# Hybrid layer on one core: 512-wide products, rests at every fourth column, low parts on GpSimd

## The chip, the core and the metric

The kernel runs on one NeuronCore of a Trainium2 chip. Its engines work side by side, each through its own queue in program order: TensorE (PE; PEld is its loading of the stationary operand), VectorE (DVE), ScalarE (ACT), GpSimd (POOL) and SyncE (SP, here only issuing DMAs). They wait for each other by semaphores. The metric is the device time of one execution in microseconds.

## What is computed

One hybrid layer on 256 tokens of width 2048, in float32. The normalised input goes through one wide projection, whose columns feed three branches; their results are gated, projected, summed, and projected once more.

```python
h = rms_norm(x, norm_g); mem_n = rms_norm(mem, mem_norm_g)
proj = h @ w_in                                   # 2048 x 20672
# split: qkv_a, z_a (1536 each), rkv_b, z_b (1536 each), lw, la (96), q_c, z_c (1024), gates (3 x 2048)
y_a = attention(q_a, k_a, v_a, rel_bias) * silu(z_a)          # 12 heads of 128, causal, with a bias by distance
y_b = rwkv7_time_mix(r_b, k_b, v_b, lw, la, ...) * silu(z_b)  # 24 heads of 64, a recurrence over the tokens
y_c = memory_cross_attention(q_c, mem_n, w_mem_kv) * silu(z_c)  # 4 heads of 256
g_a, g_b, g_c = split(sigmoid(gates), 3)
merged = g_a * (y_a @ w_proj_a) + g_b * (y_b @ w_proj_b) + g_c * (y_c @ w_proj_c)
return rms_norm(x + merged @ w_out, final_norm_g)
```

## The kernel before

**Products in two parts.** Weights and activations are float32. Each is split into a high part (fp32r) and a low part (what the high part leaves), and a product is high by high plus high by low plus low by high. Activations are kept as `[128, tile of the depth, 2, 256]`: the high and low part of 256 tokens stand next to each other.

**Jobs and chunks.** A `Job` is a product of an activation with 256 columns of a weight matrix. It goes through the depth in chunks of `KC = 4` tiles of 128 rows (512 KB). Each chunk goes through three steps, in `issue_dma` (SP loads `raw`, three buffers), `issue_split` (ACT copies the high part into `wt`, L265; VectorE subtracts to get the low part, L268; four buffers), and `products` (TensorE). `prefetch(i, ...)` keeps splits three chunks ahead of the products of chunk `i`. In mode "fm" the weights are stationary; a tile of 128 x 128 weights takes a pair: the high part by 512 columns (both parts of the activation, L303), and the low part by 256 columns (L304). In mode "tm" activations are stationary and weights stream, in the same pair. The last job of the kernel alone uses three products of 256 columns (L301). `take` adds the two halves of the bank at a job's end: ACT copies one half to `et` (L312), then VectorE or GpSimd adds.

**Lanes.** All other work (attention, the recurrence, activations) is written as generators, the lanes. After the products of each chunk `step_lanes` lets each lane issue its next piece; `yield n` is a rest of n chunks. So the program's order on every engine is set by how chunks and pieces interleave. `force` and `drain` run lanes without chunks in between, when something is needed at once or a stage ends. A lane sets flags for others, such as "attn" (the attention of a group is done) or "state_free" (the recurrent state of a group is ready).

**Stages.** The first stage (196 chunks) makes the columns for the first two branches, for six groups of two pairs of heads: jobs R, K, V, Z of the recurrence, and Q, K, Z, V of the attention. The second makes the memory branch (chunks 196 to 259), the third the gates and projections, the fourth the output. `open_p2` drains the lanes at the end of the first stage.

**The recursion.** In `rw_lane` a group needs the inverses of 8 triangular blocks per partition quadrant. Blocks go through DRAM into `NB`, and VectorE runs 31 columns, each with products (L658, into `fs_t`) and sums (L662, into `X`). A rest follows every fifth column, in which VectorE's queue gets the low part of the next chunk. Later pieces make the state, turn `YT` to tokens (L769), normalise (L772 to L798: `gn_m`, `gn_v`, square root on ACT at L134, `rs_rg`, then `Y`, with one product on GpSimd at L791), turn `Y` back (L806) and multiply into `yb`. In `attn_a` the weights of the attention are turned (L854) and copied by ACT to `pT` (L855), then multiplied with `va` (L861, L863).

## Time and profile before

| | |
|---|---|
| median of 3 runs | 1492.12 us (1491.28 to 1493.12) |
| the profiled execution | 1491.59 us, span 1489.9 us |
| TensorE busy | 1457.5 us (98%), 9083 products |
| VectorE / ACT / GpSimd busy | 981.8 / 791.3 / 199.3 us |
| low parts on VectorE (L268) | 451, 1244 ns in the mean |
| high parts on ACT (L265) | 452, 1055 ns in the mean |
| loads of weights | 448 of 512 KB and 4 of 384 KB, some 4 us from issue to landing |

A busy time is the union of an engine's instructions. Products on TensorE overlap in their records, so the step from start to start tells their pace, not the mean duration. Idle time of an engine costs only where the bounding engine waits for it. Line numbers are those of the kernel before, in the diff's removed lines and in all rows of it.

### The profile page before, as it was taken

How to read it: one execution, taken by the hardware profiler on the slowest of the kernel's cores; microseconds unless marked ns; L12 is line 12 of the kernel's file. 1: busy time of each engine (PE TensorE's matmuls, PEld its weight loads, DVE VectorE, ACT ScalarE, POOL GpSimd, SP SyncE). 2: the span in 40 equal slices, each digit the busy share in tenths (PEclk: the TensorE clock that was granted, in tenths of full speed). 3: DMA queues.
4: the chain of work that ended last, by engine and by line, in shares of the span. 5: the costliest groups of instructions: out<-in, count | busy, mean ns of one | idle time of the engine just before them, and what ended most of it. 6: DMA issues, size and time to landing. Idle time of an engine off the chain costs nothing.

```text
span 1489.9 us, 24099 instructions
## 1 busy us (share of the span) xinstructions
PE 1457.5 (98%) x9083; PEld 1249.5 (84%) x9083; DVE 981.8 (66%) x1978; ACT 791.3 (53%) x1261; POOL 199.3 (13%) x274
## 2 busy tenths in 40 slices
PE   7998999999999999999999999999999999999997
PEld 6877888888888878878888888888888888888887
DVE  5667778687786777684676655765565555555564
ACT  6535546546466366455675555654444444444453
POOL 4211222212122212112100000000000000000021
PEclk9999999999999999999999999999999999999999
DMA  6555556455555456455565555565666666666763
GB/s 188 172 172 158 157 157 169 141 159 168 145 163 170 138 150 174 132 164 168 162 223 185 170 170 170 176 192 185 189 185 191 183 186 190 189 181 189 255 208 129
DMA packets 265320, 259.00 MB, mean 174 GB/s; under 512 B 28172, under 2 KB 261284, under 8 KB 264564
## 3 DMA queue, kind: packets, MB, share of 16 engines
q1 hardware_dynamic: 261088, 248.81, 56.3%
q10 hardware_dynamic: 2292, 5.01, 0.9%
q0 software_dynamic: 1824, 3.65, 0.9%
q8 instruction: 71, 1.16, 0.3%
q14 instruction: 45, 0.37, 0.1%
HBM read 253.74 MB, written 6.05 MB: 174 GB/s over the span
## 4 chain that ended last, share of the span: by engine, by line
PE 81%; DVE 9%; DMA 5%; ACT 2%; issue 1%; SPq 1%; POOL 0%; ACTq 0%; DVEq 0%; POOLq 0%
PE pm L303 47%; PE pm L304 24%; DVE wt L268 3%; DVE fs_t L658 3%; DVE X L662 2%; PE psd L601 2%; DMA NB<-d 2%; DMA raw<-in_w_in_dram 2%; DMA fr<-fd 1%; ACT wt L265 1%; PE pm L301 1%; PE psd L1008 1%; PE psd L740 1%; DMA d<-GS 1%; PE psd L621 1%
## 5 line engine op out<-in xcount | busy, mean ns | idle before, releaser
L303 PE MATMUL pm<-hT,wt 128*128 128x512 f32 (+1 forms) x2400 | 861.2, 401 | 0.0
L268 DVE TENSOR_TENSOR wt<-raw,wt 128x1024 fp32r<-128x1024 f32 (+1 forms) x451 | 559.9, 1244 | 369.9 <-ACT wt L265 369.2
L265 ACT ACTIVATE wt<-raw 128x1024 fp32r<-128x1024 f32 (+1 forms) x452 | 475.3, 1055 | 401.5 <-PE pm L304 255.0
L304 PE MATMUL pm<-hT,wt 128*128 128x256 f32 (+1 forms) x2400 | 674.3, 281 | 11.4 <-DVE wt L268 11.4
L303 PEld LDWEIGHTS pm<-hT,wt 128*128 128x128 f32 (+1 forms) x2400 | 449.5, 187 | 115.7 <-issue 11.0
L304 PEld LDWEIGHTS pm<-hT,wt 128*128 128x128 f32 (+1 forms) x2400 | 452.3, 188 | 17.6 <-DVE wt L268 17.2
L312 ACT ACTIVATE et<-pm 128x256 f32<-128x256 f32 (+1 forms) x240 | 91.5, 383 | 135.7 <-PE pm L304 130.3
L1108 POOL TENSOR_TENSOR gtb<-gtb,gta 128x512 f32<-128x512 f32 x8 | 17.2, 2150 | 628.7 <-DVE gtb L1106 628.7
L303 PE MATMUL pm<-wt,mg 128*128 128x512 f32 x224 | 78.7, 393 | 0.0
L658 DVE TENSOR_TENSOR fs_t<-X,NB 128x30 f32<-128x30 f32 (+13 forms) x354 | 65.3, 223 | 17.2 <-DMA NB<-d 8.7
L303 PE MATMUL pm<-wt,hT 128*128 128x512 f32 x192 | 69.5, 403 | 1.1 <-DVE wt L268 1.1
L303 PE MATMUL pm<-ybs,wt 128*128 128x512 f32 x192 | 67.8, 393 | 0.0
L303 PE MATMUL pm<-yas,wt 128*128 128x512 f32 x192 | 67.7, 393 | 0.0
L304 PE MATMUL pm<-wt,mg 128*128 128x256 f32 x224 | 63.4, 283 | 0.0
L318 POOL TENSOR_TENSOR lraw<-lraw,et 128x256 f32<-128x256 f32 (+1 forms) x38 | 39.1, 1043 | 148.4 <-ACT lraw L317 147.9
L662 DVE TENSOR_TENSOR X<-X,fs_t 128x30 f32<-128x30 f32 (+13 forms) x354 | 55.2, 191 | 0.6
L304 PE MATMUL pm<-ybs,wt 128*128 128x256 f32 x192 | 54.3, 283 | 0.0
L304 PE MATMUL pm<-yas,wt 128*128 128x256 f32 x192 | 54.3, 283 | 0.0
L304 PE MATMUL pm<-wt,hT 128*128 128x256 f32 x192 | 53.7, 280 | 0.0
L303 PEld LDWEIGHTS pm<-wt,mg 128*128 128x128 f32 x224 | 42.1, 188 | 9.7
L303 PEld LDWEIGHTS pm<-wt,hT 128*128 128x128 f32 x192 | 36.0, 188 | 11.4 <-issue 2.1
L303 PE MATMUL pm<-ycs,wt 128*128 128x512 f32 x128 | 45.3, 394 | 0.0
(316 smaller groups left out, 1742.2 us busy)
## 6 DMA issues: line engine op xcount, KB each, us to landing
raw<-in_w_in_dram SPq DMA_DIRECT2D x320, 512.0 KB, 3.8
raw<-in_w_mem_kv_dram SPq DMA_DIRECT2D x32, 512.0 KB, 3.6
raw<-in_w_out_dram SPq DMA_DIRECT2D x32, 512.0 KB, 4.1
raw<-in_w_proj_a_dram SPq DMA_DIRECT2D x24, 512.0 KB, 4.4
raw<-in_w_proj_b_dram SPq DMA_DIRECT2D x24, 512.0 KB, 3.7
raw<-in_w_proj_c_dram SPq DMA_DIRECT2D x16, 512.0 KB, 4.3
NB<-d SPq DMA_DIRECT2D x24, 128.0 KB, 4.8
fr<-fd ACTq DMA_DIRECT2D x6, 385.0 KB
```

The lines of the kernel that those rows point to most:

```text
L265: act.activation(w[:, :, 0, 0:j.n], r[:, :, 0:j.n], AF.Copy)
L268: eng.tensor_tensor(w[:, :, 1, 0:j.n], r[:, :, 0:j.n], w[:, :, 0, 0:j.n].bitcast(FT), OP.subtract)
L301: pe.matmul(ps[:, 0:256], l, r, start=first and n == 0, stop=last and n == 2)
L303: pe.matmul(ps[0:j.m], hi, both, start=first, stop=last, skip_group_check=True)
L304: pe.matmul(ps[0:j.m, 256:512], lo, top, start=False, stop=last, skip_group_check=True)
L312: act.activation(t, ps[0:j.m, 256:512], AF.Copy)
L318: pool.tensor_tensor(j.dst[f], j.dst[f], t, OP.add)
L601: pe.matmul(pv[h][:, w].rearrange("p x t -> p (x t)"), BK[rows, q, c, w * 128:(w + 1) * 128], AR[rows, q, c].rearrange("p x t -> p (x t)") ...
L621: pe.matmul(pv[rows, q], tok[:, q, c, rows], GS[:, c * 4 + 2 * q + h, 2:4].rearrange("p x t -> p (x t)"), start=(c == 0), stop=True, skip_ ...
L658: dve.tensor_tensor(t, X[:, k0:8, c:c + 1].to_broadcast([128, m, hi - lo]), NB[:, lo:hi, c].rearrange("p (o n) -> p o n", o=1).to_broadcas ...
L662: dve.tensor_tensor(X[:, k0:8, lo:hi], X[:, k0:8, lo:hi], t, OP.add)
L1108: pool.tensor_tensor(g, g, gates["a"], OP.add)
```

## The change

1. A new mode "wide" with 512 columns and chunks of 2 tiles of the depth. The activation is stationary and the weights stream: three products of 512 columns (high by high, high by low, low by high) accumulate in one bank, for each half of the tokens. The values of the attention (`va`: three jobs for two groups each), those of the memory branch (`vmm`: two jobs), all gates and projections and the first 1536 columns of the output are made so. Bytes per chunk stay 512 KB, and the number of chunks stays 452.
2. Their results need no adding of halves: `va_evac`, `vmm_evac`, `gate_evac`, `proj_evac` and `out_wide` take them from the bank. Gates and projections now come with tokens on partitions; gate and projection of a branch follow each other, the sum is kept in `yb`, the gate in `ya`, and `turn_merged` turns it with eight transposes per 512 columns.
3. The recursion rests after every fourth column. While it runs, low parts of chunks with odd numbers are queued on GpSimd.
4. The order of jobs in the first two stages changes with the wide jobs; `XN` shares the buffer of `X`, `Z` that of `fs_t`.

```diff
     def issue_split(eng=dve, hold=None):
...
-        act.activation(w[:, :, 0, 0:j.n], r[:, :, 0:j.n], AF.Copy)
+        act.activation(w[:, :, 0], r, AF.Copy)
...
-                issue_split()
+                issue_split(pool if "inverse" in flags and at["split"] % 2 else dve)
...
     def products(j, ps, f, c, w):
...
-            if j is seq[-1][0]:
+            if j.mode == "wide" or j is seq[-1][0]:
                 for n, (l, r) in enumerate(((hi, w[:, k, 0]), (hi, w[:, k, 1]), (lo, w[:, k, 0]))):
-                    pe.matmul(ps[:, 0:256], l, r, start=first and n == 0, stop=last and n == 2)
+                    pe.matmul(ps[:, 0:j.n], l, r, start=first and n == 0, stop=last and n == 2)
                 continue
...
+    def va_evac(g):
+        def f(ps, t):
+            if t == 0:
+                if g:
+                    force(("attn", g - 1))
...
+            for i in range(2):
+                act.activation(St["va", g + i][:, t], two(ps)[:, i], AF.Copy)
+                if t == 1:
+                    flags["va", g + i] = True
...
         yield 2
+        flags["inverse"] = True
         for c in range(31, 0, -1):
...
-            if c % 5 == 0:
+            if c % 4 == 0:
                 yield 1
-            if c == 15:
+            if c == 16:
...
-            if c == 5:
+            if c == 8:
...
+        del flags["inverse"]
...
-    for g in range(NG):
-        r, a = RJ[4 * g:4 * g + 4], AJ[3 * g:3 * g + 3]
-        jobs += [r[0], r[1], r[2], a[0], a[1], a[2], r[3]]
-    jobs += AJ[3 * NG:-2] + [AJ[-1], AJ[-2]]
+    VJ = [Job(w_in2, VA + 512 * i, 512, 16, hT, va_evac(2 * i), mode="wide") for i in range(3)]
+    AJ = AJ[0:3] + VJ[0:1] + AJ[3:8] + VJ[1:2] + AJ[8:14] + VJ[2:3] + AJ[14:18]
+    for g, (a0_, a1_) in enumerate(((0, 3), (3, 5), (5, 8), (8, 10), (10, 13), (13, 16))):
+        jobs += RJ[4 * g:4 * g + 3] + AJ[a0_:a1_] + RJ[4 * g + 3:4 * g + 4 - (g == NG - 1)]
+    jobs += AJ[16:20] + [RJ[-1], AJ[20]]
...
+    def vmm_evac(i):
...
+            for h in range(2):
+                act.activation(St["vmm", i + h][:, t, 0], two(ps)[:, h], AF.Copy)
+            def low():
+                for h in range(2):
+                    x = St["vmm", i + h][:, t]
+                    dve.tensor_tensor(x[:, 1], two(ps)[:, h], x[:, 0].bitcast(FT), OP.subtract)
+                    if t == 1:
+                        flags["vmm", i + h] = True
+            low()
...
+    def turn_merged(c, acc):
+        yield 2
+        for i in range(0, 4, 2):
+            p = ps_side()
+            pv = p.rearrange("p (a t c) -> p a t c", a=2, t=2)
+            for a in range(2):
+                for t in range(2):
+                    pe.transpose(pv[:, a, t], acc[:, t, (i + a) * 128:(i + a + 1) * 128], ident)
+            m = E["mg"][:, 4 * c + i:4 * c + i + 2]
+            act.activation(m[:, :, 0], two(p), AF.Copy)
+            dve.tensor_tensor(m[:, :, 1], two(p), m[:, :, 0].bitcast(FT), OP.subtract)
+            yield 1
+        flags["mg", c] = True
```

**Where instructions moved.** VectorE in the first group's recursion, before: `wt` is a chunk's weights, `fs_t` and `X` are the products and sums of a column; from one low part to the next.

```order
L268 TENSOR_TENSOR wt<-raw,wt 128x4x256 x2
L658 TENSOR_TENSOR fs_t<-X,NB 128x16
L658 TENSOR_TENSOR fs_t<-X,NB 128x15
L662 TENSOR_TENSOR X<-X,fs_t 128x16
L662 TENSOR_TENSOR X<-X,fs_t 128x15
L658 TENSOR_TENSOR fs_t<-X,NB 128x15 x2
L662 TENSOR_TENSOR X<-X,fs_t 128x15 x2
L268 TENSOR_TENSOR wt<-raw,wt 128x4x256
```

VectorE at the same place after, from the second low part on: two runs of four columns with no low part between them.

```order
L273 TENSOR_TENSOR wt<-raw,wt 128x4x256
L681 TENSOR_TENSOR fs_t<-X,NB 128x28
L681 TENSOR_TENSOR fs_t<-X,NB 128x26
L685 TENSOR_TENSOR X<-X,fs_t 128x2x14
L685 TENSOR_TENSOR X<-X,fs_t 128x2x13
L681 TENSOR_TENSOR fs_t<-X,NB 128x26 x2
L685 TENSOR_TENSOR X<-X,fs_t 128x2x13 x2
L681 TENSOR_TENSOR fs_t<-X,NB 128x26
L681 TENSOR_TENSOR fs_t<-X,NB 128x24
L685 TENSOR_TENSOR X<-X,fs_t 128x2x13
L685 TENSOR_TENSOR X<-X,fs_t 128x2x12
```

The low part of every second chunk has left VectorE's queue; 21 in the six recursions stand on GpSimd.

VectorE at the end of the first stage, before: the normalisation of the last group, with low parts of weights between its steps (`rs_rg` is the reciprocal root, `Yq` the bonus).

```order
L268 TENSOR_TENSOR wt<-raw,wt 128x4x256
L142 RECIPROCAL rs_rg<-rs_sg 128x8
L143 TENSOR_TENSOR rs_sg<-rs_rg 128x8
L144 SCALAR_TENSOR_TENSOR rs_sg<-rs_sg,rs_vg 128x8
L145 SCALAR_TENSOR_TENSOR rs_rg<-rs_sg,rs_rg 128x8
L789 TENSOR_TENSOR Y<-Y,rs_rg 128x512
L793 TENSOR_TENSOR Yq<-tok,bs 128x256 x2
L268 TENSOR_TENSOR wt<-raw,wt 128x4x256 x2
L798 TENSOR_TENSOR Y<-Y,Yq 128x512
L268 TENSOR_TENSOR wt<-raw,wt 128x4x256 x2
L809 SCALAR_TENSOR_TENSOR yb<-psd,par_324,zsb 128x256 x2
```

VectorE there after; the first row is the low part of chunk 199, the last chunk split before the draining.

```order
L273 TENSOR_TENSOR wt<-raw,wt 128x4x256
L142 RECIPROCAL rs_rg<-rs_sg 128x8
L143 TENSOR_TENSOR rs_sg<-rs_rg 128x8
L144 SCALAR_TENSOR_TENSOR rs_sg<-rs_sg,rs_vg 128x8
L145 SCALAR_TENSOR_TENSOR rs_rg<-rs_sg,rs_rg 128x8
L813 TENSOR_TENSOR Y<-Y,rs_rg 128x512
L817 TENSOR_TENSOR Yq<-tok,bs 128x256 x2
L473 TENSOR_TENSOR zsa<-zsa,et 128x512
L822 TENSOR_TENSOR Y<-Y,Yq 128x512
L890 TENSOR_TENSOR ya<-psd,zsa 128x512
L833 SCALAR_TENSOR_TENSOR yb<-psd,par_324,zsb 128x256 x2
```

No low parts are left between the steps: the whole rest of the normalisation stands in the draining.

ACT at the same place, before (the last chunks of the first stage; `et` and `zsa` are copies at the end of the last job).

```order
L312 ACTIVATE et<-pm 128x256
L317 ACTIVATE zsa<-pm 128x256
L312 ACTIVATE et<-pm 128x256
L317 ACTIVATE zsa<-pm 128x256
L855 ACTIVATE pT<-psd 128x384 x2
L265 ACTIVATE wt<-raw 128x4x256
```

ACT there after.

```order
L317 ACTIVATE et<-pm 128x256
L322 ACTIVATE zsa<-pm 128x256
L317 ACTIVATE et<-pm 128x256
L322 ACTIVATE zsa<-pm 128x256
L134 ACT_TABLE_LOAD
L134 ACTIVATE rs_sg<-gn_v,epsc 128x8
L879 ACTIVATE pT<-psd 128x384 x2
L270 ACTIVATE wt<-raw 128x4x256
```

The table and the square root of the normalisation came to stand between the last copies and `pT`.

## Rows read from the trace of the kernel before

**Rows 1.** The page: engines' busy time (part 1), and a group of part 5.

```profile
PE 1457.5 (98%) x9083; PEld 1249.5 (84%) x9083; DVE 981.8 (66%) x1978; ACT 791.3 (53%) x1261; POOL 199.3 (13%) x274
...
L265 ACT ACTIVATE wt<-raw 128x1024 fp32r<-128x1024 f32 (+1 forms) x452 | 475.3, 1055 | 401.5 <-PE pm L304 255.0
```

**Rows 2.** Waits of TensorE: us in total, times, longest.

```profile
PE pm L304 <- DVE wt L268: 11.4, 16, 1.6
```

**Rows 3.** Lines 303 (952 to 1469 us) and 301: durations, first and last start.

```profile
L303 PE MATMUL pm<-wt,mg x223: 387/396/398, 1391.0 to 1469.0; 128*128 128x512 f32 x112
...
L301 PE MATMUL pm<-wt,mg x96: 281/284/286, 1469.7 to 1481.1; 128*128 128x256 f32 x96
```

**Rows 4.** TensorE in order of time, second stage: start, duration, instruction.

```profile
771.69 0.39 PE L303 MATMUL pm<-hT,wt 128*128 128x512 f32 x1
771.92 0.28 PE L304 MATMUL pm<-hT,wt 128*128 128x256 f32 x1
772.04 0.60 PE L154 MATMUL psd<-ident,m_sb 128*128 128x128 f32 x4
772.39 0.48 PE L303 MATMUL pm<-hT,wt 128*128 128x512 f32 x1
772.71 0.28 PE L304 MATMUL pm<-hT,wt 128*128 128x256 f32 x1
772.83 0.40 PE L303 MATMUL pm<-hT,wt 128*128 128x512 f32 x1
```

**Rows 5.** A recursion's window: us; PE, PEld, DVE, ACT, POOL busy (count); PEclk, DMA. Low parts.

```profile
219.00:245.00 26.00, 24.74 (x145) 20.74 (x144) 25.63 (x131) 13.44 (x27) 3.90 (x7) 1.00 0.59 164
...
L268 DVE TENSOR_TENSOR wt<-raw,wt 128x1024 fp32r<-128x1024 f32 x6 | 7.3, 1216 | 0.0
```

**Rows 6.** Another recursion in order of time, on GpSimd and VectorE.

```profile
551.97 1.57 POOL L318 TENSOR_TENSOR zsb<-zsb,et 128x256 f32<-128x256 f32 x2 [14.28 <-ACT zsb L317]
...
552.17 1.45 DVE L658 TENSOR_TENSOR fs_t<-X,NB 128x35 f32<-128x35 f32 x2
553.55 0.31 DVE L662 TENSOR_TENSOR X<-X,fs_t 128x35 f32<-128x35 f32 x2
553.77 0.35 DVE L658 TENSOR_TENSOR fs_t<-X,NB 128x35 f32<-128x35 f32 x2
...
555.70 1.23 DVE L268 TENSOR_TENSOR wt<-raw,wt 128x1024 fp32r<-128x1024 f32 x1
```

**Rows 7.** GpSimd's sums and differences of two tensors, by time and by line.

```profile
44.71 1.04 POOL L427 TENSOR_TENSOR et<-lraw 128x512 f32<-128x512 f32 x1
...
L268 POOL TENSOR_TENSOR wt<-raw,wt 128x768 fp32r<-128x768 f32 x1 | 1.8, 1849 | 5.2 <-ACT wt L265 5.2
```

**Rows 8.** End of the first stage: TensorE and ACT by time, groups of 725 to 748 us.

```profile
741.59 0.82 PE L854 MATMUL psd<-ident,as 128*128 128x128 f32 x6
...
744.21 0.48 PE L303 MATMUL pm<-hT,wt 128*128 128x512 f32 x1
...
742.07 0.38 ACT L317 ACTIVATE zsa<-pm 128x256 f32<-128x256 f32 x1
742.33 0.88 ACT L855 ACTIVATE pT<-psd 128x384 f32<-128x384 f32 x2
...
L793 DVE TENSOR_TENSOR Yq<-tok,bs 128x256 f32<-128x256 f32 x2 | 1.9, 968 | 0.0
L791 POOL TENSOR_TENSOR Y<-Y,lnw 128x512 f32<-128x512 f32 x1 | 1.4, 1408 | 3.9 <-DVE Y L789 3.9
L134 ACT ACT_TABLE_LOAD x1 | 1.3, 1283 | 0.0
L789 DVE TENSOR_TENSOR Y<-Y,rs_rg 128x512 f32<-128x512 f32 x1 | 0.7, 694 | 0.0
L134 ACT ACTIVATE rs_sg<-gn_v,epsc 128x8 f32<-128x8 f32 x1 | 0.3, 300 | 0.0
L142 DVE RECIPROCAL rs_rg<-rs_sg 128x8 f32<-128x8 f32 x1 | 0.2, 193 | 0.0
```

More of the change, by code (lines that the diff above doesn't have):

```diff
@@ L289, in products @@
         a = j.a() if callable(j.a) else j.a
-        for k in range(KC):
-            kt = c * KC + k
+        for k in range(j.kc):
+            kt = c * j.kc + k
             first, last = kt == 0, kt == j.kt - 1
@@ L333, in issue_mm @@
             j.pre(c)
[L334 removed]
+        end = c == j.kt // j.kc - 1
         w = wts.pop(i)
@@ L353, in issue_mm @@
             if end:
-                take(j, j.ps[f], f)
+                if j.mode == "wide":
+                    j.evac(j.ps[f], f)
+                else:
+                    take(j, j.ps[f], f)
     def two(p):
@@ L987, in f @@
             return [t[:, 0], t[:, 1]], got
+        return f
+    def vmm_evac(i):
+        def f(ps, t):
+            if t == 0:
+                for h in range(2):
+                    St["vmm", i + h] = E["aw"].tile([128, 2, 2, 256], FR, name="vmm", bufs=2)
+            for h in range(2):
+                act.activation(St["vmm", i + h][:, t, 0], two(ps)[:, h], AF.Copy)
+            def low():
+                for h in range(2):
+                    x = St["vmm", i + h][:, t]
[3 more added lines that the diff above has]
+            low()
         return f
@@ L1064, in tile_hybrid @@
     kj = [Job(wm2, 256 * i, 256, 16, lambda: E["mT"], c_evac("kmm", i, "aw")) for i in range(4)]
-    vj = [Job(wm2, 1024 + 256 * i, 256, 16, lambda: E["mT"], c_evac("vmm", i, "aw"), mode="tm") for i in range(4)]
+    vj = [Job(wm2, 1024 + 256 * i, 512, 16, lambda: E["mT"], vmm_evac(i), mode="wide") for i in (0, 2)]
     zj = [Job(w_in2, ZC + 256 * i, 256, 16, hT, zc_evac(i)) for i in range(4)]
     zj[0].before, kj[0].before = open_p2, start_c
-    jobs += zj[0:3] + [qj[0], kj[0], vj[0], qj[1], kj[1], vj[1], qj[2], kj[2], vj[2], qj[3], kj[3], vj[3], zj[3]]
+    jobs += zj[0:3] + [qj[0], kj[0], qj[1], kj[1], vj[0], qj[2], kj[2], qj[3], kj[3], vj[1], zj[3]]
     s3 = ExitStack()
@@ new lines, in proj_evac, with evac @@
+    def proj_evac(nm, c):
+        def evac(ps, f):
+            g = gates["g"][:, f]
+            if nm == "a":
+                if f == 0:
+                    force("ybs")
+                    gates["acc"] = quad(yb, c % 2)
+                dve.tensor_tensor(gates["acc"][:, f], ps, g, OP.mult)
+                return
+            acc = gates["acc"]
+            dve.tensor_tensor(g, ps, g, OP.mult)
+            dve.tensor_tensor(acc[:, f], acc[:, f], g, OP.add)
+            if nm == "c" and f == 1:
+                add_lane(turn_merged(c, acc))
+        return evac
@@ L1185, in tile_hybrid @@
     wo = w_out[0]
-    jobs += [Job(wo, c * 256, 256, 16, lambda: E["mg"], out_evac(c), mode="out", before=(open_p4 if c == 0 else None))
-             for c in range(8)]
+    jobs += [Job(wo, c * 512, 512, 16, lambda: E["mg"], out_wide(c), mode="wide", before=(open_p4 if c == 0 else None),
+                 pre=(lambda k: force(("mg", 3)) if k == 6 else None) if c == 0 else None) for c in range(3)]
+    jobs += [Job(wo, c * 256, 256, 16, lambda: E["mg"], out_evac(c), mode="out") for c in (6, 7)]
     for j in jobs:
-        for c in range(j.kt // KC):
+        for c in range(j.kt // j.kc):
             seq.append((j, c))
```

82 lines of the change are left out of this document (43 added, 39 removed).

## The prediction

> **What bounds the kernel now.** I read the shares of the engines first. TensorE is busy for 98% of the span [rows 1], and the span is 1489.9 us of a run of 1491.59 us, so 1.7 us lie around it. The view of its waits names one waiting that counts: 11.4 us in 16 pieces for low parts made by VectorE [rows 2]. So nearly all of the time is TensorE going through its columns, and an edit is worth what it takes out of that stream or puts into it.
>
> Then the pace of the stream. In the last stage 223 pairs of a 512-wide and a 256-wide product start between 1391.0 and 1469.0 us: 78.0/222 = 0.3514 us a pair of 768 columns. The last job has 96 products of 256 columns in a row, 11.4/95 = 0.120 us each [rows 3]. Inside a pair the step after the 512-wide one is 0.23 us and the step after the 256-wide one 0.12 us [rows 4]. The granted clock is 1.00 of full speed [rows 5], the level of 2.4 GHz, at which the columns alone would take 768/2.4 = 320 ns; the pair carries 0.031 us on top.
>
> Third, the recursion (six times, once per group). In 219 to 245 us VectorE is busy 25.63 of 26.0 us while TensorE does some seven chunks of weights [rows 5]: here, and only here, VectorE is the slower one, and the waits of rows 2 come from it.
>
> **The change part by part.** *Wide products.* The jobs that change are, counted in 256 columns by 16 tiles of the depth, 6 for va, 4 for vmm, 24 gates, 16 projections (8 x 32 tiles) and 6 of the output: 56, or 448 blocks of 128 x 512 weights. Each goes from four pairs to six 512-wide products; the columns are 3072 in both. Four pairs are 4 x 0.3514 = 1.406 us. A 512-wide product next to another does not occur before. By difference it is 0.3514 - 0.120 = 0.2314 us, six are 1.388 us, and the gain is 0.0175 x 448 = 7.8 us. Bounds: if what a pair carries on top is the same for every product (0.0157 us), six cost 1.374 and the gain is 14 us; if it goes by columns, six cost 1.406 and the gain is 0. I take 8, which lies between and rests on a row for the nearest form.
>
> The Trainium skill (TensorE: Matmul & The Clock Gate, section Back-to-back issue gap) puts the step between warm products at N/2.4 + 2.5 ns, 216 ns for 512 columns; by that six are 1.295 us and the gain would be 50 us. The trace disagrees at the one place where it can: the step after a 512-wide product is 0.23 us [rows 4].
>
> *Turning the merged result.* It now comes out with tokens on partitions and is turned by 32 transposes, eight groups of four. Such a group stands between two pairs at 772.04 us. From 771.69 to 772.83 us there are two pairs and one group: 1.14 - 0.70 = 0.44 us [rows 4]. Eight cost 3.5 us on TensorE, and since nothing there waits otherwise they stand in the sum: +4 (3.5 to 5).
>
> *The recursion.* A column costs VectorE (555.70 - 553.77)/4 = 0.48 us [rows 6], a low part 1.22 us [rows 5]. Other work of VectorE in the 26 us is about 26.0 - 31 x 0.48 - 7.3 = 3.8 us, some 0.5 us a chunk. Before, a chunk brings 5 columns and a low part: 2.4 + 1.2 + 0.5 = 4.1 us. TensorE needs eight pairs for it, 2.8 us, and small products: of its 145 in the window [rows 5] seven chunks have 112, and the 33 others at 0.1 us (a quarter of the 0.44 above) add 0.4 a chunk, so 3.2 us. VectorE falls back by 0.9 us a chunk over 6.5 chunks, 5.9 us, and the three chunks of lead swallow most of that.
>
> After, two chunks bring 8 columns (3.9), one low part on VectorE (1.2) and other work (1.0), 6.1 us against 6.4 on TensorE. If GpSimd's low part cost VectorE nothing, the waits would be gone. But it costs. At 551.97 us two sums on GpSimd run for 1.57 us, and two of VectorE's products, begun at 552.17, take 1.45 us in place of 0.35, the next starting at 553.55 when GpSimd ends [rows 6]: VectorE's operations with both inputs in SBUF stand still meanwhile. The page SBUF — State Buffer of the Trainium skill (Who interferes with whom) says the same as a rule, an exclusive lock; the sum here goes by the row.
>
> A low part of 128 x 1024 on GpSimd isn't in the trace. 128 x 512 alone takes 1.04 us and 128 x 768, partly disturbed, 1.85 us [rows 7], so 2.0 to 2.5 us; a bit less of it blocks, and I take 1.8. Then two chunks are 7.9 us, and VectorE falls back by 0.75 us a chunk over nearly eight chunks: 5.9 us a group, as much as before. The low part costs VectorE more on GpSimd (1.8) than at home (1.2), and the more frequent rest gives that back.
>
> Two groups are worse than that. Group 0 starts late and puts 4 columns, not 2, ahead of the first low part: +1 us. In group 2 the code forces two steps of the lanes at once (the attention buffer is still held), so the recursion is queued two chunks early and its wait for its data holds the low parts behind it: +2 us. Together I take +3 for the term. Bounds: -11 (all waits of rows 2 gone) to +14 (2.4 us blocked, four times in six groups).
>
> *The end of the first stage.* The order of jobs moves the recursions of the last groups back by one step each and some by more. In program order the last group's state is ready four chunks later than before, while the first stage ends at the same chunk (195). So the normalisation of the last group falls into the draining of the lanes, where no weights stand between its steps. Before, from the end of chunk 195 to the first product of chunk 196 pass 744.21 - 741.59 = 2.62 us [rows 8].
>
> After, in order from the end of the chunk:
> - ACT's last copies are done after 0.86 us, and the table and the square root take 1.28 + 0.30, to 2.4 us;
> - pT comes behind them on ACT, 0.88, to 3.3;
> - the high part for chunk 199 takes 1.06 [rows 1], to 4.4, and its low part 1.2 on VectorE, to 5.6;
> - the reciprocal and three small ones come only then, 4 x 0.2, to 6.4; Y by rstd 0.69, to 7.1;
> - Yq beside GpSimd's product takes 1.86, to 9.0; the silu of zsa and the sum, 0.69 each, to 10.4;
> - four transposes end near 10.8 us [rows 8].
>
> That is 8 us more with TensorE idle for some 6 of them. Bounds: 3 (the chain starts earlier, because VectorE and ACT are ahead of TensorE) to 12 (the granted clock falls in the idle stretch; no row shows it fall inside the span).
>
> *Evacuation of the wide values.* va and vmm are marked ready as soon as their last copy is queued, not some steps later, so the attention products that stand next on TensorE wait for one or two copies of 128 x 256 (0.38 us on ACT [rows 8], about the same on VectorE): once in the first stage, twice in the second, and once more in the forced steps. I put 2.5 us (0 to 4).
>
> *At nothing:* fewer copies and sums on ACT, VectorE and GpSimd in the wide jobs, longer runs per weight row in the loads, the shared buffers of XN and Z. ACT, VectorE and the loads are hidden by TensorE outside the recursion; the waits of rows 2 name none of them. If the cover were gone, an evacuation would cost about its copy, 0.4 us per job.
>
> **Sum:** -8 + 4 + 3 + 8 + 2.5 = +9.5 us on the profiled 1491.6, so 1501 us; the median of the runs is 0.5 us above the profiled run, so I say 1501.5 us.
>
> **The rivals.** (A) *The recursion's waits vanish.* GpSimd's low parts fall into stretches in which VectorE has no recursion to do: before its data have landed, or in its waits. For it: half of the low parts no longer stand behind columns. Against it: VectorE has only 0.4 idle of 26 us there [rows 5]. The term is then -11 in place of +3: 1501.5 - 14 = 1487.5, faster than before. The point from which it decides: less than 0.3 us blocked by a low part (6.1 against 6.4 us).
>
> (B) *A 512-wide product costs its columns.* All of the 0.031 us of a pair would come from the 256-wide product, which is too short to hide the next load of weights. Then six cost 6 x 0.2133 = 1.280 us, and the gain is 0.126 x 448 = 56 us: about 1453 us. The rule of the skill named above ends near it. Against it: 0.23 us for the step after the 512-wide one, and three 256-wide ones carry only 0.013 us each.
>
> (C) *GpSimd's low part costs more*, 2.4 us blocked or late behind its other work, and TensorE's clock falls in the drain: 1501.5 + 11 + 4 = 1516.
>
> (D) *The drain is hidden* (+3) and the wide products gain 14: 1501.5 - 5 - 6 = 1490.5, no change that can be told.
>
> **How the numbers follow.** Forecast 0.58, A 0.13, B 0.05, C 0.13, D 0.11. A measurement of this kernel can tell about 0.2% (3 us) from no change. Faster by more than that: most of A (0.10), B, a third of D (0.04): 0.19. Within 0.2%: the rest of A (0.03), most of D (0.07) and a small part of the forecast (0.05): 0.15. Slower: 0.66. The forecast's own range from its terms is 1493 to 1511. To hold 8 in 10 it reaches down over D into A, 1485, and up towards C, 1513; B stays out.
>
> **What would show it.** In the profile after: the step between 512-wide products of the wide jobs, 0.231 us if I am right, 0.216 if B. Waits of TensorE for wt in the recursions: 11 to 17 us in total, with both VectorE and GpSimd as makers, and VectorE's small products stretched to near 2 us where GpSimd makes a low part. A gap of some 6 us on TensorE before the last four transposes of Y. What would make it wrong: that gap being absent, or the waits in the recursions gone.

## The result, and the profile after

The changed kernel takes 1508.62 us (median of four runs, 1507.77 to 1510.81) against 1492.28 us of the kernel before: a ratio of 1.011, 95% interval 1.0096 to 1.0124. It is 16 us slower. The profiled run has a span of 1507.0 us against 1489.9.

In the page after, part 1 and the groups of the two operations of a column and of GpSimd's low parts (before, one column operation took 223 ns on L658 and 191 ns on L662 in the mean; the 22 include one of the first job):

```profile
PE 1459.7 (97%) x8219; PEld 1215.6 (81%) x8219; DVE 962.8 (64%) x1847; ACT 753.4 (50%) x1127; POOL 228.8 (15%) x273
...
L681 DVE TENSOR_TENSOR fs_t<-X,NB 128x30 f32<-128x30 f32 (+13 forms) x354 | 89.6, 292 | 12.2 <-DMA NB<-d 11.8
L685 DVE TENSOR_TENSOR X<-X,fs_t 128x30 f32<-128x30 f32 (+13 forms) x354 | 73.4, 242 | 0.6
L273 POOL TENSOR_TENSOR wt<-raw,wt 128x1024 fp32r<-128x1024 f32 (+1 forms) x22 | 54.5, 2476 | 76.8 <-ACT wt L270 70.5
```

Against [rows 1]: TensorE has 864 products fewer (9083 to 8219), and is busy 2.2 us longer. It idles 47.3 us instead of 32.4. The waits of TensorE after (us in total, times, longest), the counterpart of [rows 2]:

```profile
PE pm L309 <- DVE wt L273: 10.6, 8, 2.9
...
PE psd L885 <- ACT pT L879: 5.9, 3, 3.6
PE psd L830 <- DVE Y L822: 5.5, 1, 5.5
PE psd L729 <- ACT Z L720: 3.3, 2, 2.4
```

The waits for low parts are no longer in total than before, 10.6 against 11.4 us. But they come in 8 pieces instead of 16, and the longest is 2.9 us. (Left out is a load at the start, of 9 us, which both kernels have.) The attention's weights (L885), the last transposes (L830) and the inverse's small products (L729, and L741 with 0.8 us) are new as waits. Of the 5.9 us on L885, 2.1 stand in the draining at the end of the first stage.

**The clock.** What the page's busy time hides is the granted clock. The view of windows after (us; busy time of PE, PEld, DVE, ACT, POOL with counts; PEclk, DMA share, GB/s):

```profile
134.00:137.20 3.20, 0.31 (x3) 0.06 (x1) 3.20 (x10) 3.20 (x7) 2.38 (x3) 1.00 0.00 0
137.30:140.60 3.30, 3.30 (x11) 2.81 (x12) 3.30 (x12) 0.36 (x1) 3.12 (x4) 0.50 0.58 167
140.80:146.00 5.20, 5.20 (x31) 4.52 (x30) 5.03 (x29) 2.14 (x3) 0.00 (x0) 1.00 0.60 160
...
270.40:273.70 3.30, 3.30 (x12) 2.77 (x11) 2.98 (x4) 2.47 (x5) 2.85 (x5) 0.50 0.34 96
355.80:359.00 3.20, 3.20 (x12) 2.71 (x12) 3.20 (x25) 0.53 (x1) 0.00 (x0) 0.50 0.55 164
485.50:488.70 3.20, 3.20 (x13) 2.69 (x11) 2.28 (x4) 3.07 (x5) 3.07 (x5) 0.50 0.40 133
581.10:584.30 3.20, 3.20 (x11) 2.66 (x11) 3.03 (x10) 1.27 (x2) 0.91 (x2) 0.50 0.00 1
764.80:768.60 3.80, 3.80 (x14) 3.22 (x13) 0.88 (x2) 0.00 (x0) 0.00 (x0) 0.50 0.39 65
```

Read the first three together. From 134.0 to 137.2 TensorE does 0.31 us of work while it waits for a low part. Then for 3.3 us its clock is at half, 1.2 GHz, and it is "busy" with only 11 products; after that it is back at 2.4 GHz. Five such stretches of 3.3 us or a little more lie in the first stage, and one begins in the draining at its end. In the kernel before the clock was 1.00 up to the tail of the run. Five stretches at half clock cost 5 x 1.7 = 8.5 us, and the part of the sixth behind the draining some 2 more; none of it shows as a wait.

The last long wait ahead of each of the other four stretches (TensorE in order of time; the brackets hold the idle time and what ended it):

```profile
268.37 1.00 PE L729 MATMUL psd<-XT,Z 32*32 32x32 f32 x29 [2.41 <-ACT Z L720]
...
354.81 0.38 PE L309 MATMUL pm<-hT,wt 128*128 128x256 f32 x1 [2.09 <-DVE wt L273]
...
484.07 1.00 PE L729 MATMUL psd<-XT,Z 32*32 32x32 f32 x29 [0.92 <-ACT Z L720]
...
580.38 0.70 PE L885 MATMUL psd<-pT,va 128*128 128x256 f32 x2 [3.58 <-ACT pT L879]
```

So two of the five stretches stand behind waits for low parts (137 and 356 us), and three behind waits of other lanes for ACT.

**By stage**, from the starts of the first product of chunks 196 (second stage) and 260 (third):

| | before | after | difference |
|---|---|---|---|
| first stage, up to chunk 196 | 744.21 | 764.79 | +20.6 |
| second stage, 196 to 260 | 196.4 | 200.1 | +3.6 |
| third and fourth, to the end of the span | 549.3 | 542.2 | -7.1 |

So the wide products gain where they stand alone, and the first stage loses three times that. Of the 3.6 us of the second stage some 2 are half clock behind the draining; the rest is not explained here.

**The pace of the wide products**: TensorE in order of time, a job of gates and a projection.

```profile
964.85 21.97 PE L306 MATMUL pm<-wt,hT 128*128 128x512 f32 x96
986.66 0.64 PE L306 MATMUL pm<-wt,yas 128*128 128x512 f32 x2
...
1025.22 16.91 PE L306 MATMUL pm<-wt,ybs 128*128 128x512 f32 x72
1041.96 0.87 PE L306 MATMUL pm<-wt,hT 128*128 128x512 f32 x3
...
1080.38 0.60 PE L1156 MATMUL psd<-ident,yb 128*128 128x128 f32 x4
1080.74 3.00 PE L306 MATMUL pm<-wt,hT 128*128 128x512 f32 x12
1083.58 0.60 PE L1156 MATMUL psd<-ident,yb 128*128 128x128 f32 x4
```

A gate job takes (986.66 - 964.85)/96 = 0.2272 us a product, a projection (1041.96 - 1025.22)/72 = 0.2325. Before, pairs of gates in the third stage (line 303, 1007 to 1030 us; durations, first and last start) went at 22.2/63 = 0.352 us, projections at 0.351:

```profile
L303 PE MATMUL pm<-hT,wt x64: 395/398/403, 1007.7 to 1029.9; 128*128 128x512 f32 x64
```

From one group of four transposes to the next pass 1083.58 - 1080.38 = 3.20 us, with 12 products between them, which take 12 x 0.2272 = 2.73. So a group costs 0.47 us, eight of them 3.8.

**The end of the first stage** after (the counterpart of [rows 8]), engines in order of time:

```profile
754.09 0.82 PE L878 MATMUL psd<-ident,as 128*128 128x128 f32 x6
...
756.47 0.85 ACT L879 ACTIVATE pT<-psd 128x384 f32<-128x384 f32 x2
...
758.30 1.23 DVE L273 TENSOR_TENSOR wt<-raw,wt 128x1024 fp32r<-128x1024 f32 x1 [3.87 <-ACT wt L270]
...
760.88 1.82 DVE L817 TENSOR_TENSOR Yq<-tok,bs 128x256 f32<-128x256 f32 x2
...
764.05 1.09 PE L830 MATMUL psd<-ident,Y 128*128 128x128 f32 x4 [5.48 <-DVE Y L822]
764.79 0.78 PE L308 MATMUL pm<-hT,wt 128*128 128x512 f32 x1
```

From the end of chunk 195 to the first product of chunk 196 pass 10.7 us, against 2.62 before.

### The profile page after: what moved, and what is told of

Same layout as the page of the kernel before. It is cut to its first block, busy times and chain, and to the rows that moved or that the text cites. A ratio compares the mean times of both kernels' runs of the same rounds, so it can differ in the third digit from the quotient of the medians.

```text
span 1507.0 us, 21991 instructions
## 1 busy us (share of the span) xinstructions
PE 1459.7 (97%) x8219; PEld 1215.6 (81%) x8219; DVE 962.8 (64%) x1847; ACT 753.4 (50%) x1127; POOL 228.8 (15%) x273
## 3 DMA queue, kind: packets, MB, share of 16 engines
q0 software_dynamic: 1824, 3.65, 0.9%
## 4 chain that ended last, share of the span: by engine, by line
PE 78%; DVE 11%; DMA 6%; ACT 3%; issue 1%; SPq 1%; POOL 0%; DVEq 0%; ACTq 0%
PE pm L306 40%; PE pm L308 19%; PE pm L309 9%; DVE fs_t L681 4%; DMA raw<-in_w_in_dram 3%; DVE X L685 3%; DVE wt L273 2%; PE psd L623 2%; ACT wt L270 1%; DMA NB<-d 1%; DMA fr<-fd 1%; PE psd L1051 1%; PE psd L764 1%; DMA x_sb<-in_x_dram 1%; PE psd L154 0%
## 5 line engine op out<-in xcount | busy, mean ns | idle before, releaser
L308 PE MATMUL pm<-hT,wt 128*128 128x512 f32 (+1 forms) x1632 | 598.6, 408 | 1.2 <-ACT wt L270 1.0
L309 PE MATMUL pm<-hT,wt 128*128 128x256 f32 (+1 forms) x1632 | 461.5, 283 | 10.6 <-DVE wt L273 10.6
L308 PEld LDWEIGHTS pm<-hT,wt 128*128 128x128 f32 (+1 forms) x1632 | 309.6, 190 | 83.8 <-issue 7.3
L306 PE MATMUL pm<-wt,hT 128*128 128x512 f32 x1440 | 335.6, 391 | 0.0
L309 PEld LDWEIGHTS pm<-hT,wt 128*128 128x128 f32 (+1 forms) x1632 | 311.3, 191 | 13.5 <-DVE wt L273 13.1
L306 PEld LDWEIGHTS pm<-wt,hT 128*128 128x128 f32 x1440 | 268.5, 188 | 59.0 <-issue 2.6
L681 DVE TENSOR_TENSOR fs_t<-X,NB 128x30 f32<-128x30 f32 (+13 forms) x354 | 89.6, 292 | 12.2 <-DMA NB<-d 11.8
L306 PE MATMUL pm<-wt,mg 128*128 128x512 f32 (+1 forms) x384 | 79.3, 367 | 0.0
L306 PEld LDWEIGHTS pm<-wt,mg 128*128 128x128 f32 x384 | 65.7, 189 | 12.5
L685 DVE TENSOR_TENSOR X<-X,fs_t 128x30 f32<-128x30 f32 (+13 forms) x354 | 73.4, 242 | 0.6
L306 PE MATMUL pm<-wt,yas 128*128 128x512 f32 x288 | 67.6, 395 | 0.0
L306 PE MATMUL pm<-wt,ybs 128*128 128x512 f32 x288 | 67.6, 395 | 0.0
L273 POOL TENSOR_TENSOR wt<-raw,wt 128x1024 fp32r<-128x1024 f32 (+1 forms) x22 | 54.5, 2476 | 76.8 <-ACT wt L270 70.5
L306 PEld LDWEIGHTS pm<-wt,ybs 128*128 128x128 f32 x288 | 54.3, 188 | 12.6
```

Source lines behind the costliest of these rows:

```text
L273: eng.tensor_tensor(w[:, :, 1], r, w[:, :, 0].bitcast(FT), OP.subtract)
L306: pe.matmul(ps[:, 0:j.n], l, r, start=first and n == 0, stop=last and n == 2)
L308: pe.matmul(ps[0:j.m], hi, both, start=first, stop=last, skip_group_check=True)
L309: pe.matmul(ps[0:j.m, 256:512], lo, top, start=False, stop=last, skip_group_check=True)
L681: dve.tensor_tensor(t, X[:, k0:8, c:c + 1].to_broadcast([128, m, hi - lo]), NB[:, lo:hi, c].rearrange("p (o n) -> p o n", o=1).to_broadcas ...
L685: dve.tensor_tensor(X[:, k0:8, lo:hi], X[:, k0:8, lo:hi], t, OP.add)
```

## Taking the recursion's change apart

The recursion has two edits: the rest after every fourth column, and low parts on GpSimd. My theory after the result (theory 1) was that a low part on GpSimd takes more from VectorE than it spares it, and that the long waits behind it bring the clock down. Rival 2 was that GpSimd does help and something else spoils it; rival 3, that the loss comes from the new order of jobs and the draining.

**Without GpSimd.** In `prefetch` of the changed kernel:

```
-                issue_split(pool if "inverse" in flags and at["split"] % 2 else dve)
+                issue_split()
```

> The changed kernel with all low parts on VectorE again; rest after every fourth column, wide products and job order stay. Theory 1 (a low part on GpSimd holds VectorE's columns up for some 2.1 us, more than the 1.2 us that it saves there; the few long waits that follow bring the granted clock down to half): a chunk brings VectorE 4 columns (1.9), a low part (1.2) and other work (0.5), 3.65 us against 3.2 on TensorE, so the waits for low parts fall from 10.6 to about 4 us and the stretches of half clock in the recursions, five of 3.4 us, mostly vanish: 1508.6 - 6 - 7 = about 1495 us. The drain at the end of the first stage stays as it is. Rival 2 (GpSimd relieves VectorE as intended): VectorE falls further back, the waits grow by the 0.6 us a chunk more: 1512 us or above.

Measured: 1488.33 us, 0.9974 of before (0.9963 to 0.9984), 7 us below what theory 1 gave. Twenty microseconds hang on 21 low parts. Its waits of TensorE:

```profile
PE pm L309 <- DVE wt L273: 3.5, 4, 2.3
```

The waits for low parts fell to 3.5 us, as the count of VectorE's work (3.65 us a chunk against 3.2) had said, and those of other lanes shrank with them (L885, L729 and L741 from 10.0 to 5.4 us). None of the five stretches at half clock is left; one stands at another place, behind the wait of 2.3 us in the first recursion. Rival 2 falls. All of the gain lies ahead of the draining: chunk 195 ends at 733.5 us instead of 754.1. The draining stayed, 10.7 us from there to the first product of chunk 196, with the clock at half in it and for 3.5 us behind it.

**The old rest, with GpSimd.** In the recursion of the changed kernel:

```
-            if c % 4 == 0:
+            if c % 5 == 0:
...
-            if c == 16:
+            if c == 15:
...
-            if c == 8:
+            if c == 5:
```

> The changed kernel with the rest after every fifth column as before; low parts of odd chunks stay on GpSimd. The shorter count of rests also puts the last group's normalisation back among the chunks before the end of the first stage. Theory 1 (GpSimd's low parts cost VectorE 2.1 us each): two chunks bring 10 columns (4.8), one low part (1.2), 2.1 of standing still and 1.0 other work, 9.1 us against 6.4: the waits grow by some 2 us a group, +12 us, more half clock, +3, and the drain gives 8 back: about 1515 us. Rival 3 (the loss is the drain and the job order, not the recursion): 1508.6 - 9 = about 1499 us.

Measured: 1503.93 us (ratio 1.0081, 1.0063 to 1.01). Waits for low parts doubled, to 20.1 us in 9 pieces, the longest 6.0, as theory 1 said. But those on L729 and L741, and the long one on L885, went, so that chunk 195 ends only 3.0 us later (757.1 us). The draining fell from 10.7 to 2.8 us and gave back more than that. So the time lies between the two expectations: both theories had a part of it.

**The old recursion.** Both edits above together.

> The changed kernel with the recursion as before (rest after every fifth column, all low parts on VectorE); wide products and job order stay, and the last group's normalisation is back among the chunks. Theory 1 (the long waits in the recursions and the drain are the loss): no half clock in the recursions (-8.5), the drain back near 2.6 us (-8 to -10), waits for low parts about 11 us in small pieces: about 1491 us. Rival 3 (half clock and waits come with the job order, the forced steps and the turning of pieces): about 1499 us, with half clock still in several groups.

Measured: 1483.23 us, 0.9937 of before (0.9923 to 0.9952): the lowest time of all kernels run here (the intervals of the next three, 1484.1 to 1485.2 us, overlap with its own), and faster than both theories said. Its waits:

```profile
PE pm L309 <- DVE wt L273: 7.4, 11, 1.6
...
PE psd L830 <- DVE Y L822: 1.3, 2, 1.0
```

No stretch of half clock before the tail. Rival 3 falls for the greater part: the new order of jobs with the wide products is a gain by itself. By stage the traces show -4.1 us up to chunk 196, +3.0 in the second stage (199.4 us, of which TensorE idles 2.1) and -7.1 in the last two. What the wide `va` and what the new order add to the first stage was not separated.

Between this run and the changed kernel the recursions can be told from the draining: chunk 195 ends at 737.3 and at 754.1 us, 16.8 us apart, and the draining takes 2.8 and 10.7 us.

**The recursion's change in the kernel before.** The reverse: `before.py` with all of the recursion's edits and nothing else.

```
-                issue_split()
+                issue_split(pool if "inverse" in flags and at["split"] % 2 else dve)
...
+        flags["inverse"] = True
...
-            if c % 5 == 0:
+            if c % 4 == 0:
...
```

> The kernel before with the recursion's change alone: rest after every fourth column and low parts of odd chunks on GpSimd while it runs; no wide products, old job order. Theory 1: waits about as long in total as before (11 us) but in fewer, longer pieces, and after the longest of them a stretch at half clock, 1.7 us each, in three to five groups: 1492.3 + 6 to 9 = about 1500 us. Rival 2 (the recursion's change is a gain by itself, and the wide jobs' order spoils it): 1482 to 1488 us.

Measured: 1515.03 us (1.0155, 1.014 to 1.0171). The sign was right, the size was 23 us and not 8; the clock was at half in six stretches of the first stage. So I took its halves too.

**The rest alone, in the kernel before**: only the lines with `c`.

> The kernel before with the rest after every fourth column and nothing else (all low parts on VectorE, no wide products). Theory 1 (the more frequent rest gains and GpSimd's low parts lose): a chunk brings VectorE 3.65 us against 3.2 on TensorE, waits for low parts fall from 11.4 to about 4 us, a stretch or two of half clock after the longest (1.7 us each), and the longer recursions put the last normalisation a chunk or so later (+2): 1492.3 - 7.5 + 2 + 2 = about 1489 us. Rival (the rest costs by itself: a step more per group, the drain as long as in the changed kernel): 1495 us or above.

Measured: 1502.55 us (1.0068, 1.0053 to 1.0083). Theory 1 failed, and the rival's 1495 us or above came. The waits of TensorE:

```profile
PE pm L304 <- DVE wt L268: 6.2, 7, 2.1
PE psd L705 <- ACT Z L696: 3.4, 2, 2.8
PE psd L806 <- DVE Y L798: 2.7, 1, 2.7
```

The waits for low parts did shrink, to 6.2 us. In their place came others, which the kernel before hardly has: the inverse's small products for ACT (L705), the transposes of Y for VectorE (L806, 4.9 us in two waits). Chunk 195 ends 7.3 us later than before (748.8 against 741.6), with one stretch of half clock from 265.0 to 271.8 us, and the draining takes 6.0 us instead of 2.6. My reading is that a rest more per group moves the pieces of all lanes against the chunks, and that in this order of jobs they meet badly; no run tests it by itself. Of that I had priced only the draining.

**GpSimd alone, in the kernel before**: only the line in `prefetch` and the flag.

> The kernel before with the low parts of odd chunks on GpSimd while the recursion runs and nothing else. Theory 1: as between the two runs of the changed kernel with a rest of five (1503.9 against 1483.2), some 20 us are lost: 1512 us, with waits of 5 us and more for low parts and half clock after them. Rival (the loss needs the new order of jobs or the new rest): 1495 to 1500 us.

Measured: 1523.34 us (1.0207, 1.019 to 1.0224): theory 1 held in kind, and the loss is 31 us and not 20. The clock is at half in seven stretches, and the waits are

```profile
PE pm L304 <- DVE wt L268: 30.0, 13, 6.0
```

The two squares side by side (us):

| | all low parts on VectorE | odd ones on GpSimd | difference |
|---|---|---|---|
| order of after, rest 5 | 1483.2 | 1503.9 | +20.7 |
| order of after, rest 4 | 1488.3 | 1508.6 | +20.3 |
| order of before, rest 5 | 1492.3 | 1523.3 | +31.0 |
| order of before, rest 4 | 1502.6 | 1515.0 | +12.5 |

GpSimd's low parts cost 12 to 31 us wherever they are put. The rest of four costs 5 us in the new order and 10 in the old one, and gains 8 only in the one case where VectorE is furthest behind. In the new order the 5 us are not lost in the recursions: with all low parts on VectorE, chunk 195 ends 3.8 us earlier with the rest of four (733.5 against 737.3), and then the draining takes 7.9 us more, with half clock behind it. In the old order chunk 195 itself ends later (748.8 against 741.6).

## Why a low part on GpSimd costs so much

The trace of the changed kernel, GpSimd and VectorE in order of time in the first recursion:

```profile
127.87 2.50 POOL L273 TENSOR_TENSOR wt<-raw,wt 128x1024 fp32r<-128x1024 f32 x1 [7.36 <-ACT wt L270]
128.02 2.58 DVE L681 TENSOR_TENSOR fs_t<-X,NB 128x40 f32<-128x40 f32 x2
...
130.74 0.35 DVE L681 TENSOR_TENSOR fs_t<-X,NB 128x36 f32<-128x36 f32 x2
...
135.86 1.23 DVE L273 TENSOR_TENSOR wt<-raw,wt 128x1024 fp32r<-128x1024 f32 x1
136.00 3.32 POOL L273 TENSOR_TENSOR wt<-raw,wt 128x1024 fp32r<-128x1024 f32 x1 [0.82 <-ACT wt L270]
137.01 2.39 DVE L681 TENSOR_TENSOR fs_t<-X,NB 128x36 f32<-128x36 f32 x1
137.15 0.50 PE L309 MATMUL pm<-hT,wt 128*128 128x256 f32 x1 [2.89 <-DVE wt L273]
```

Two products of a column, 0.35 us at 130.74, take 2.58 beside GpSimd's low part at 127.87. At 136.00 it is the other way round: GpSimd begins behind VectorE's low part and takes 3.32. The same two operations of a column in the run with the old recursion:

```profile
L681 DVE TENSOR_TENSOR fs_t<-X,NB 128x30 f32<-128x30 f32 (+13 forms) x354 | 64.5, 222 | 13.9 <-POOL zsa L323 7.8
L685 DVE TENSOR_TENSOR X<-X,fs_t 128x30 f32<-128x30 f32 (+13 forms) x354 | 55.5, 192 | 0.6
```

In the changed kernel they are busy for 89.6 + 73.4 = 163.0 us in all groups, here for 64.5 + 55.5 = 120.0: 43 us for 21 low parts, 2.0 us each, to spare 1.22.

And the wait of 2.89 us at 137.15 shows how the pieces became long: with every second low part elsewhere, VectorE's own low part of chunk 34 stands behind eight columns, one of them stretched to 1.42 us by another sum on GpSimd. To test the standing still, GpSimd's subtraction was replaced by a copy of the raw weights:

```
-            eng.tensor_tensor(w[:, :, 1], r, w[:, :, 0].bitcast(FT), OP.subtract)
+            if eng is pool and j.kt == 16 and i > 8:
+                eng.tensor_copy(w[:, :, 1], r)
+            else:
+                eng.tensor_tensor(w[:, :, 1], r, w[:, :, 0].bitcast(FT), OP.subtract)
```

> The changed kernel with what GpSimd does for odd chunks replaced by a copy of the raw weights (one input from SBUF in place of two; the low parts of these 21 chunks are then wrong). Order, waits and buffers stay. Theory 1 (the loss comes from VectorE's two-input operations standing still while GpSimd reads two inputs): the columns run at their own pace, two chunks bring VectorE 6.1 us against 6.4 on TensorE, waits for low parts fall from 10.6 to about 2 us, the stretches of half clock in the recursions go: 1508.6 - 8 - 7 - 3 (waits of other lanes) = about 1490 us; the drain stays. Rival 4 (the loss comes from GpSimd being slow or its queue being late, whatever it reads): about 1505 us, and VectorE's columns as stretched as before.

Measured: 1486.48 us (0.9955, 0.9938 to 0.9971). The time is near what theory 1 said, its wording was not. Waits for low parts fell to 5.2 us (2 were expected), and no stretch at half clock is left ahead of the draining. The trace of this run, same recursion:

```profile
132.55 1.04 POOL L274 CAST wt<-raw 128x1024 fp32r<-128x1024 f32 x1
132.60 1.14 DVE L688 TENSOR_TENSOR X<-X,fs_t 128x35 f32<-128x35 f32 x2
```

VectorE stands still beside a copy with one input just as well: two sums take 1.14 us beside a copy of 1.04 (0.32 us without GpSimd in the changed kernel, at 133.08). It is only shorter, 1.19 us in the mean instead of 2.48. (18 of the 21 copies met a column; the column operations are 12 us longer than in the run with the old recursion, 0.6 us a copy.) Since the copy is also the shorter work for GpSimd, the time alone would fit rival 4, a slow GpSimd, as well; that VectorE stands still is told by the rows, and the columns are stretched much less than before, which rival 4 had excluded. The Trainium skill (SBUF — State Buffer, Who interferes with whom) says it so: an operation of VectorE with two inputs in SBUF contends with any operation of GpSimd that reads SBUF. These rows agree; my "two inputs on both sides" was narrower than they are. What counted in these two runs is how long GpSimd reads.

## Whether idleness brings the clock down

If the stretches at half clock come from the waits ahead of them, filling the waits with work must remove them, although no wait is shorter. The changed kernel with extra products right before its long waits:

```
+    FILL = {30: 10, 34: 12, 90: 9}
...
+            if k == 0 and f == 0:
+                for _ in range(FILL.get(cur[0], 0)):
+                    pe.matmul(ps[0:j.m], zero[:, 0:j.m], both, start=False, stop=False, skip_group_check=True)
...
+        fill(p, {1: 10, 3: 4}.get(g, 0))
...
+        fill(p, 22 if g == NG - 1 else 0)
...
+        fill(p, {3: 14, 5: 9}.get(g, 0))
```

> The changed kernel with extra products on TensorE right ahead of its long waits: 9 to 12 of them (with a zero operand, into the same bank) in chunks 30, 34 and 90, 4 to 22 (overwritten later) ahead of the late matrix pieces of groups 1 and 3, of the attention of groups 3 and 5 and of the last transposes. They fill waiting time, and no wait is taken away. Theory A (the granted clock falls to half behind a long idle stretch of TensorE): the stretches at 137, 270, 356, 485, 581 and 762 us are gone and the time falls by what they cost, 5 x 1.7 + 2 to 3: about 1498 us. Rival B (the half clock belongs to something else than idleness, such as the load of the other engines): the stretches stay, 1508 to 1511 us.

Measured: 1504.27 us (1.0073, 1.0058 to 1.0088). The windows of that run at the same places:

```profile
134.00:144.00 10.00, 9.32 (x48) 7.39 (x46) 10.00 (x47) 5.27 (x11) 5.91 (x6) 1.00 0.47 131
266.00:274.00 8.00, 8.00 (x87) 6.61 (x86) 3.82 (x5) 7.44 (x15) 5.62 (x7) 1.00 0.46 131
355.00:360.00 5.00, 5.00 (x29) 4.42 (x30) 4.96 (x35) 2.12 (x2) 0.00 (x0) 1.00 0.37 107
485.00:489.00 4.00, 4.00 (x33) 3.36 (x33) 3.31 (x4) 2.88 (x6) 3.22 (x6) 1.00 0.51 149
580.00:586.00 6.00, 6.00 (x36) 5.29 (x35) 5.83 (x20) 2.94 (x5) 0.34 (x2) 1.00 0.44 107
755.00:770.00 15.00, 14.61 (x79) 12.25 (x78) 9.33 (x15) 4.75 (x5) 1.41 (x1) 1.00 0.51 176
```

The clock is 1.00 in all six places, and nowhere in the run below it but at the tail: theory A is shown, with products by zero as well as with others. The other runs agree: the mean granted clock is 0.997 to 0.999 in all four of this kernel and 0.989 to 0.992 in all four of the changed one. The time fell by 4 us and not by 10. TensorE's idle time fell by 16.0 us (47.3 to 31.3), and its busy time rose by 11.3 (1459.7 to 1471.0) for 90 products of about 0.22 us, 20 us. So the clock gave back some 8.5 us, and some 4 us of the extra products stuck out beyond the waits that they were to fill.

How long a wait must be isn't settled. One of 2.4 us that ended at 118.3 us had no half clock behind it in the changed kernel; nearly the same one in the run without GpSimd had, from 119.7 to 122.9 us. One of 3.2 us, ended at 247.3 us in the run with the old rest and GpSimd, had none either, while the stretch at 485 us follows only 0.9 us of waiting, ahead of the inverse's small products.

## The draining and the late stages

**The last group with the old rest.** The run without GpSimd, with `n = 5 if g == NG - 1 else 4` and the rest at `c % n == 0`:

> All low parts on VectorE, rest after every fourth column in groups 0 to 4, and after every fifth in the last group, which puts its normalisation back among the chunks before the end of the first stage. Theory 1 (the run without low parts on GpSimd has 5 us of waiting for the last transposes, 10 us at half clock and 8 us more from chunk 192 to 196 than needed): 1488.3 - 10 = about 1479 us, better than the run with the old recursion (1483.2), since the waits for low parts stay at 3 to 4 us. Rival (the last group's waits come back and the drain shifts to the attention): 1485 to 1489 us.

Measured: 1484.68 us (0.9947, 0.9932 to 0.9962), 3.6 us better than without GpSimd alone, not 10; the rival's 1485 to 1489 us is as near. The draining takes 7.0 us, against 10.7 without GpSimd alone and 2.8 in the run with the old recursion, and 3.4 us of waiting for the last transposes remain. I read that from the order, and did not test it, as the rest of four in groups 0 to 4 having by then moved the last group back, a step per group. The kernel does not beat the old recursion (1483.2).

**Wide products in the last two stages alone**: first and second stage with the jobs and the recursion of before.

```
-    VJ = [Job(w_in2, VA + 512 * i, 512, 16, hT, va_evac(2 * i), mode="wide") for i in range(3)]
...
-    vj = [Job(wm2, 1024 + 256 * i, 512, 16, lambda: E["mT"], vmm_evac(i), mode="wide") for i in (0, 2)]
+    vj = [Job(wm2, 1024 + 256 * i, 256, 16, lambda: E["mT"], c_evac("vmm", i, "aw"), mode="tm") for i in range(4)]
```

> Wide products in the third and fourth stage alone (gates, projections, output); first and second stage, their order of jobs and the recursion as before. Theory: the gain of the run with the old recursion, 8.8 us, is the wide products less the transposes; by the stretch after chunk 260 (540.7 us before, some 533.8 in the run with the old recursion) 7 us of it are here: 1492.1 - 7 = about 1485 us. Rival (the gain comes from the new order in the first stage): about 1490 us.

Measured: 1485.16 us (0.995, 0.9935 to 0.9965). As expected, and the rival's 1490 us did not come: 7 to 8 of the 9 us of the old recursion's run are here.

**High parts first.** The run with the old recursion, with the products of a chunk in another order:

```
-        for f in range(2):
+        for f in range(4):
+            part, f = f // 2, f % 2
...
-            products(j, j.ps[f], f, c, w)
+            products(j, j.ps[f], f, c, w, part)
...
```

> The run with the old recursion (1483.2 us) with another order within a chunk: TensorE first does all products with the high part of the chunk's weights, for both halves, and then those with the low part, so the low part is wanted some 1.6 us later. Theory 1 (what is left in the recursions is waiting for low parts, 7.4 us in 11 pieces of at most 1.6 us): nearly all of it goes: 1483.2 - 6 = about 1477 us; if a run of 512-wide products and one of 256-wide ones also step faster than pairs (0.229 + 0.120 against 0.351 us), up to 4 us more. Rival (VectorE sets the pace there, and the wait only moves to a later chunk): 1482 to 1484 us.

Measured: 1484.06 us (0.9945, 0.993 to 0.996): no gain, as the rival said. Waits for low parts halved, and others came:

```profile
PE pm L313 <- DVE wt L273: 3.5, 4, 1.6
PE psd L722 <- DMA XN<-d: 2.7, 2, 1.7
```

Behind the new waits for `XN` (the result of the recursion, read back from DRAM) the clock was at half twice, some 3.4 us. TensorE idles 31.2 us here and 31.8 in the run with the old recursion. That fits the rival: in the recursion VectorE sets the pace, and a later need only moves the wait to the next thing that depends on it.

## Why the prediction was right, and where not

Forecast were 1501.5 us (1485 to 1513) and slower; measured 1508.6. The sum came within 7 us because two misses of opposite sign met, which is luck; the direction rests on the recursion and the draining, and both went the way that was forecast.

- **What bounds the kernel**: as said. All of the difference is TensorE's idle time (+14.9 us) and its busy time (+2.2), and the latter hides a gain of products and a loss of clock of about 10 us each.
- **Wide products, -8.** The term was right in sign and too small, by the step that it chose. Forecast was 0.231 us from one 512-wide product to the next; the gates show 0.2272, the projections 0.2325. Before, the gates' pairs went at some 0.352 us, so their 1152 products gain 1152 x (4/6 x 0.352 - 0.2272) = 8.6 us by themselves, the 768 of the projections 768 x (4/6 x 0.351 - 0.2325) = 1.2. The bound of 14 holds. The rule of the Trainium skill that stood in the prediction (TensorE: Matmul & The Clock Gate, Back-to-back issue gap: 0.216 us) is 0.011 us below the fastest row. Rival B did not come.
- **Transposes, +4**: 3.8 measured, as forecast. With the wide term, the last two stages gained 7.1 us in the trace where the sum had some 2 to 3.
- **The recursion, +3.** Here the prediction was right in the mechanism and wrong in its price: 16.8 us, by the end of chunk 195 in the changed kernel and in the run with the old recursion. GpSimd's low part takes 2.48 us (forecast 2.0 to 2.5) and stops VectorE for 2.0 (1.8); the waits for low parts stay as long in total, 10.6 against 11.4. But they were valued at their length. The step that failed is "5.9 us a group, as much as before": before, it was 16 pieces of up to 1.6 us with no half clock; after, 8 of up to 2.9, with half clock behind two of them. And other lanes wait on ACT behind the same late work: L885, L729 and L741 together 10.0 us, of which the prediction had only the 2.1 for `pT` in the draining; behind these waits stand the other three stretches. With all low parts on VectorE and nothing else changed these waits are 5.4 us and the five stretches are gone (one other came). The five cost 8.5 us, and I had put a falling clock only into the draining. From the run with the old recursion to the changed one these terms are: idle time +15.5 (low and high parts 3.8, the three lines some 10, the last transposes 4.2, others some -2), busy time +9.8, together 25 us, where recursion and draining stood with 11.
- **The rest gives it back**: half true. The count for four columns and a low part (3.65 us) was right, as the run without GpSimd shows; in the new order chunk 195 then ends 3.8 us earlier, and the 5 us lost are the draining, which the sum had. That in the old order the rest costs 7.3 us ahead of the draining was not foreseen.
- **The draining, +8**: right, nearly to the step. Forecast were 10.8 us from the end of chunk 195 to the end of the transposes; measured are 10.7, in the order given: table, `pT`, high part (757.2 us), low part, reciprocal, Y (760.3 us), Yq. TensorE idles for 7.6 us of them, not some 6. The clock then costs 2 us more, which the bound of 12 had allowed.
- **Evacuation, +2.5**: wrong place. The memory branch waits 0.5 us for its values. The long wait in the forced steps is 3.6 us, for `pT` on ACT (L885), not for `va`.
- **Rivals.** A (no waits) fell. C named the mechanism, GpSimd dearer and the clock down, but in the drain alone; the truth lies between forecast and C. D fell: the draining was not hidden.
- **The signs.** The gap before the last transposes (5.5 us, forecast some 6) and the stretched products came. The waits for low parts are just below the 11 to 17 us forecast, and all of them are for VectorE's, none for GpSimd's.

Summed up: without the recursion's change and the draining my terms give 1491.6 - 8 + 4 + 2.5 = 1490; measured 1483.2, 7 us better. With them I added 11 and measured 25, 14 us worse. The total was 7 us off.

## What to carry to other kernels

Price a wait on TensorE by its length and by what follows it: a few long waits can cost more than many short ones of the same sum, since the clock may go to half behind them. Before work is moved from VectorE to GpSimd, compare how long GpSimd will read SBUF with what VectorE saves, if VectorE works meanwhile on two inputs from SBUF. And when a schedule is shifted by a step, look at where all the other pieces land, not only those that it was shifted for.

## What the hardware showed that I had not expected

- TensorE's clock fell to 1.2 GHz for 3.3 us and more behind waits of 2.1 to 3.6 us, and once behind 0.9 us; behind others of 2.4 and 3.2 us it did not. Filling the waits with products, by zero or not, kept it at 2.4 GHz in all six places.
- The step between 512-wide products differs between jobs: 0.2272 us with `hT` stationary (gates), 0.2325 with `ybs` (projection). Why was not tried.
- GpSimd's copy of 128 x 1024 with one input (1.04 us) stops VectorE as its subtraction does; and VectorE's low part delays GpSimd's in turn (3.32 instead of 2.50 us).
